# Sample retention in a two-layer decode step: outer products on 128 zero-padded rows, fp32 old-state outputs of four batches side by side

## The chip, the cores and the metric

The kernel runs on one core of a Trainium2 chip. The metric is device time in microseconds (us), the median of several runs of the whole program. TensorE (PE) multiplies, ScalarE (ACT), VectorE (DVE) and GpSimd (POOL) work on elements, SyncE (SP) issues the DMAs.

## The reference, cut to what matters

One step of a hybrid decoder: 512 prompt tokens of one sequence and 8 sample sequences (batches) of 8 tokens each, model width 1024, two layers. Layer 0 mixes tokens by retention with 4 heads, key width 256, value width 512. Both layers then do cross-attention into 256 memory tokens and a gated ConvFFN.

For the 8 sample batches, the chunk is the 8 tokens, and each batch and head has an old state `s` of 256 x 512:

```python
scores = jnp.einsum('bhqd,bhkd->bhqk', qc, kc) * inner
o = jnp.einsum('bhqk,bhkv->bhqv', scores, vc) + jnp.einsum('bhqd,bhdv->bhqv', qc * q_dec, s)
s = s * c_dec + jnp.einsum('bhkd,bhkv->bhdv', kc * k_dec, vc)
```

The output `o` is normalised over its 512 values, multiplied by a gate and projected. The new states go back to memory. So each head reads 8 x 256 x 512 floats (4 MB) of state and writes as many. All results are fp32.

## The kernel before, in words

**Precision.** An fp32 operand is split into a high and a low part in the reduced format F32R (`split`, L190: a cast on ACT, a subtraction on DVE or POOL). A product is three matmuls: high x high, high x low, low x high (`mm3`, L185). Matmuls of plain fp32 operands exist too, in cross-attention's `stacked` (L995) and in the broadcast of the norm's scales.

**Order of the work.** PE runs one main stream of weight tiles (`project`, `run_tasks`): each tile of 512 KB is loaded by SP, cast on ACT, its rest subtracted on DVE, and used by 48 matmuls of 288 columns, shown as `acc<-xhl,wh` and `acc<-xhl,wl`. All else is a side generator that the class `Weave` (L86) puts between steps of the main stream. Weave keeps a planned time `now`: each matmul adds its columns / 2340 us, at least 0.107 (L179), and a side that yields `d` is taken up again when `now` has grown by `d` since it was last resumed; the matmuls of the side itself count as part of that. `join` runs a side to its end at once. PE, ACT, DVE, POOL and SP each take their instructions in the order in which this writes them.

**A head of retention** (`head_tasks`, L750): two weight tiles each for queries and keys, four tiles for values, four for the gate. After the keys `keys_side` (L584) turns them and makes the masked sample scores `As`; after the values `mid_side` (L622) makes the prompt's state, gathers keys and values of the samples with a selection matrix into `kst` and `vst` (L638 to L645) and makes the prompt's score products (`khl` by `qhl`, L653). It starts `b_side` (L660) for the samples. After the gate `out_side` (L710) makes the prompt's outputs. The next head's key evacuation joins both of them (L774) and writes the decayed sample queries to `Z` (L775). For the last head, the output projection joins them (L854).

**`b_side`** takes the 16 half states of a head (8 batches, two key halves of 128) in the order u = 2 b + k2. `load` fetches a half state of 128 x 512 into one of 7 buffers `S`, six ahead. `prep` splits it: cast `Sh` on ACT (L192), rest `Sl` on POOL (L193), two ahead. Per update there are three matmuls: the outer product of 8 tokens' keys and values, which stand on 32 rows of `kst`/`vst` (24 rows carry the three products of the split, row strip 32 g) (L695), and `Z` times `Sh` and times `Sl` into one output `pso` (L697). `Z` has 128 columns per update: 64 of the high part, 64 of the low, all zero but for the batch's own tokens. Then DVE makes the new state in place (L699) and SP stores it (L700); the side yields 1.9. The outputs thus stand on 128 partitions, high and low, are added (L703, L704), normalised on 64 rows and handed to `gate_out` (L569).

PSUM has four one-bank buffers `tp` for all sides in this stage, and two larger ones for the main stream.

Of the kernel before, what the change touches and what calls it, by code (L numbers as in the profile page):

```python
# [135 lines left out]
def body(ctx, tc, a, cdec):  # L136
# [4 lines left out]
    def f(t):  # L141
        return t.bitcast(F32)
# [393 lines left out]
    xs = new(ap1, [128, KT, 128], "xs", F32R)  # L536
    for hl in range(2):
        pool.tensor_copy(xs[:, :, 64 * hl:64 * hl + 64], f(xhl[:, hl, :, 0:NS]))
    Z = new(ap, [128, 2, 1088], "Z", F32R)
    pool.memset(f(Z), 0.0)  # L540
    Zv = Z.rearrange("p k (b s) -> p k b s", s=136)
    AOFF = (0, 512, 896, 1152)
    hd = [dict() for _ in range(H)]
    y3 = {}

    def rope_evac(i, ps, s):
        p = flat(ps)
# [18 lines left out]
        rstd_pow(rs[:rows], mv[:rows, 1:2], 1, rows, ap, 1.0, GN_EPS)  # L566
        return mv, rs

    def gate_out(h, on, rows, c0):  # L569
        ps = tp()  # L570
        sg = hd[h]["sg"]
        for i in range(4):
            transpose(ps[:, rows * i:rows * (i + 1)], on[:rows, 128 * i:128 * i + 128], ident[:rows, :rows])
        y = new(ap, [128, 4, 128], "yt", bufs=2)
        dve.tensor_tensor(out=y[:, :, :rows], in0=ps[:, :4 * rows].rearrange("p (i t) -> p i t", i=4),
                          in1=sg[:, :, c0:c0 + rows], op=ALU.mult)
        if h < 3:
            dma.dma_start(out=y_dram[:, 4 * h:4 * h + 4, c0:c0 + rows], in_=y[:, :, :rows])
        else:
            for i2 in range(2):  # L580
                t = y3[i2]
                split(t[:, 0, :, c0:c0 + rows], t[:, 1, :, c0:c0 + rows], y[:, 2 * i2:2 * i2 + 2, :rows])

    def keys_side(h):  # L584

        s = hd[h]
        r, khl, qhl = s["rk"], s["khl"], s["qhl"]
        yield 4.5
        ks = new(ap, [128, 2, 128], "ks", F32R)
        for hl in range(2):  # L590
            pool.tensor_copy(ks[:, :, 64 * hl:64 * hl + 64], f(khl[:, hl, :, 0:NS]))
        s["kt_s"] = kt_s = new(ap, [NS, 2, 256], "kt_s", F32R)
        ps = tp()
        for k2 in range(2):
            transpose(ps[:NS, 128 * k2:128 * k2 + 128], r[:, k2, 0:NS], ident)
        split(kt_s[:, 0], kt_s[:, 1], ps[:NS, 0:256], scale=tab[:NS, 528 + h:529 + h])
        yield 1.0
        s["kd"] = kd = new(ap1, [128, 2, 4, 256], "kdA", F32R)
        for c2 in range(2):
            ps = tp()  # L600
            for j in range(2):
                c = 2 * c2 + j
                for k2 in range(2):
                    transpose(ps[:, 256 * j + 128 * k2:256 * j + 128 * k2 + 128],
                              r[:, k2, NS + 128 * c:NS + 128 * c + 128], ident)
            for j in range(2):
                c = 2 * c2 + j
                split(kd[:, 0, c], kd[:, 1, c], ps[:, 256 * j:256 * j + 256],
                      scale=tab[:, 512 + 4 * h + c:512 + 4 * h + c + 1])
            yield 1.5  # L610
        ps = tp()
        for k2 in range(2):
            for hl in range(2):
                mm(ps[:, :NS], ks[:, k2], qhl[:, hl, k2, 0:NS], k2 + hl == 0, k2 + hl == 2)
        t1 = new(ap, [NS, NS], "sc1", bufs=2)
        act.copy(t1, ps[64:128, :NS])
        dve.tensor_tensor(out=t1, in0=ps[0:64, :NS], in1=t1, op=ALU.add)
        dve.tensor_tensor(out=t1, in0=t1, in1=tab[:NS, 256 + 64 * h:320 + 64 * h], op=ALU.mult)
        s["As"] = As = new(ap, [NS, 128], "As", F32R)
        split(As[:, 0:64], As[:, 64:128], t1)  # L620

    def mid_side(h):  # L622

# [3 lines left out]
        for k2 in range(2):  # L627
            ps = tp()
            for c in range(4):
                cc = slice(128 * k2, 128 * k2 + 128)  # L630
                mm3(ps, kd[:, 0, c, cc], kd[:, 1, c, cc], vhl[:, 0, c], vhl[:, 1, c], c == 0, c == 3)
                yield 0.0
            sp = new(ap, [128, DV], "S", bufs=7)
            act.copy(sp, ps)
            dma.dma_start(out=a["o_ret_p"][0, 0, h, 128 * k2:128 * k2 + 128], in_=sp)
        s["kst"] = kst = new(ap, [128, 2, 256], "kst", F32R)
        s["vst"] = vst = new(ap, [128, 2, DV], "vst", F32R)
        for w, (src, dst, n) in enumerate(((kt_s, kst, 256), (vs, vst, DV))):  # L638
            for j in range(2):
                ps = tp()  # L640
                rr = slice(32 * j, 32 * j + 32)
                for hl in range(2):
                    mm(ps[:, :n], sel[rr, 2 * w + hl], src[rr, hl], hl == 0, hl == 1)
                act.copy(dst[:, j], ps[:, :n])
            yield 0.5  # L645
        s["bl"] = wv.spawn(b_side(h), 0.5)
        s["A"] = A = new(ap1, [128, 2, 1280], "kdA", F32R)
# [12 lines left out]
    def b_side(h):  # L660

        s = hd[h]
        As, vs, kst, vst = s["As"], s["vs"], s["kst"], s["vst"]
        S, hl_ = {}, {}

        def state(t, u):
            return t[0, u // 2, h, 128 * (u % 2):128 * (u % 2) + 128]

        def load(u):
            if u < 2 * B:  # L670
                S[u] = new(ap, [128, DV], "S", bufs=7)
                dma.dma_start(out=S[u], in_=state(a["state_ret"], u))

        def prep(u):
            if u < 2 * B:
                hl_[u] = [new(ap, [128, DV], t, F32R, bufs=3) for t in ("Sh", "Sl")]
                split(*hl_[u], S[u], lo_pool=True)

        for u in range(7 - 1):
            load(u)  # L680
        yield 3.5
        prep(0)
        yield 1.0
        prep(1)
        pso = tp()
        for hl in range(2):
            mm(pso, As, vs[:, hl], hl == 0, False)
        yield 0.3
        for u in range(2 * B):
            load(u + 7 - 1)  # L690
            prep(u + 2)
            b, k2 = divmod(u, 2)
            g, j = b % 4, b // 4
            psu = tp()
            mm(psu, kst[32 * g:32 * g + 32, j, 128 * k2:128 * k2 + 128], vst[32 * g:32 * g + 32, j], True, True)  # L695
            for i, t in enumerate(hl_.pop(u)):
                mm(pso, Z[:, k2, 128 * b:128 * b + 128], t, False, u == 2 * B - 1 and i == 1)  # L697
            Su = S.pop(u)
            dve.scalar_tensor_tensor(out=Su, in0=Su, scalar=cdec[h], in1=psu, op0=ALU.mult, op1=ALU.add)  # L699
            dma.dma_start(out=state(a["o_ret_s"], u), in_=Su)  # L700
            yield 1.9
        t0 = new(ap, [NS, DV], "At", bufs=2)
        act.copy(t0, pso[64:128])  # L703
        dve.tensor_tensor(out=t0, in0=pso[0:64], in1=t0, op=ALU.add)  # L704
        mv, rs = gn_stats(t0, NS)
        dve.tensor_scalar(out=t0, in0=t0, scalar1=mv[:NS, 0:1], scalar2=rs[:NS], op0=ALU.subtract, op1=ALU.mult)
        yield 5.5
        gate_out(h, t0, NS, 0)

    def out_side(h):  # L710

        s = hd[h]
        A, vhl = s["A"], s["vhl"]
        ons = {}
        for qc in range(5):
            if qc < 4:
                ps = tp()
                for kc in range(qc + 1):
                    o = AOFF[kc] + 128 * (qc - kc)
                    mm3(ps, A[:, 0, o:o + 128], A[:, 1, o:o + 128], vhl[:, 0, kc], vhl[:, 1, kc], kc == 0, kc == qc)  # L720
                mv, rs = gn_stats(ps, 128)
                ons[qc] = on = new(ap, [128, 512], "on", bufs=2)
                nb = new(ap, [128, 1], "gn_nb", bufs=3)
                dve.tensor_scalar(out=nb, in0=mv[:, 0:1], scalar1=rs, scalar2=-1.0, op0=ALU.mult, op1=ALU.mult)
                act.activation(on, ps, AF.Identity, scale=rs, bias=nb)
                yield 6.0
            if qc > 0:
                gate_out(h, ons.pop(qc - 1), 128, NS + 128 * (qc - 1))
                yield 0.5

    def xk0(kt):
# [18 lines left out]
    def head_tasks(h):  # L750
# [16 lines left out]
        def ev_k(i, ps):  # L767
            rope_evac(i, ps, sk_)
            if i == 1:
                s["rk"] = sk_["r"]  # L770
                s["khl"] = khl = new(ap1, [128, 2, 2, NT], "khl", F32R)
                split(khl[:, 0], khl[:, 1], sk_["r"])
                if h > 0:
                    wv.join(hd[h - 1]["bl"], hd[h - 1]["out"])  # L774
                split(Zv[:, :, :, 0:8], Zv[:, :, :, 64:72], s["tq"].rearrange("p k (b t) -> p k b t", t=T))  # L775
                s["keys"] = wv.spawn(keys_side(h))

        tasks = project([(w_in, 256 * h), (w_in, 256 * h + 128)], xk0, ev_q)
# [1 line left out]
        for kp in range(4):  # L780
            def run(wt, kp=kp):
# [29 lines left out]
                t0 = new(ap, [NS, DV], "At", bufs=2)  # L811
                act.copy(t0, pvs[64:128])
                dve.tensor_tensor(out=t0, in0=pvs[0:64], in1=t0, op=ALU.add)
                split(vs[:, 0], vs[:, 1], t0, scale=rtok[:NS, 0:1])
                s["mid"] = wv.spawn(mid_side(h), 1.5)
                if h == 3:
                    s["y2"] = wv.spawn(y2_side())
# [652 lines left out]
```

## Time and profile before

| | us |
|---|---|
| median of three runs | 1966.99 (1962.16 to 1967.77) |
| the profiled execution | 1960.34 |
| its span, first to last instruction | 1958.5 |
| PE busy in the span | 1905.7 |
| DVE, ACT, POOL busy | 1095.6, 757.0, 400.9 |

A row of a timeline gives the start, the time to the end of the last of its instructions, engine, line of the helper that records the instruction (L176 for matmuls, L182 for transposes, L192 and L193 for splits), operation, out<-in by tile names, partitions x columns, and the count. Matmuls overlap, so the cost of one to the stream is read from the distance of starts, not from its duration. A stationary operand is written as rows*columns (32*128: 32 rows, 128 output columns).

### The profile page before, as it was taken

The page shows a single profiled execution, that of the slowest core. Times are in us where ns is not written, and L with a number is a line of the kernel's source. Part 1 is how long each engine was busy: PE and PEld are TensorE (multiplying, and loading weights), DVE is VectorE, ACT ScalarE, POOL GpSimd, SP SyncE. Part 2 cuts the span into 40 slices and gives each one's busy share as a digit, 9 for nine tenths or more (in the row PEclk, how much of TensorE's full clock was granted, in tenths as well). Part 3 has the DMA queues.
Part 4 walks back from the last instruction along what each step waited for, and adds up shares of the span by engine and source line. Part 5 has one row for each costly group of instructions (what it writes and reads, how often), then busy time and mean ns, then how long its engine had stood idle before and what let it go on. Part 6 is the DMA issues. An engine that isn't in the chain of part 4 may idle for free. (4 is left out here: it accounts for less than half of the span.)

```text
span 1958.5 us, 32666 instructions
## 1 busy us (share of the span) xinstructions
PE 1905.7 (97%) x13341; PEld 1772.8 (91%) x13341; DVE 1095.6 (56%) x1651; ACT 757.0 (39%) x1142; POOL 400.9 (20%) x491
## 2 busy tenths in 40 slices
PE   7999999999999999999999999978999999999998
PEld 5888888888899989899999999858888999999998
DVE  4645546354542554576366356696545664564467
ACT  5443342434522434443134234435443432342235
POOL 0123142231400321221011011354212110110010
PEclk9999999999999999999999999989999999999999
DMA  8635363454642464323222222446453332222224
GB/s 276 204 115 187 91 204 109 147 156 145 213 147 87 151 200 147 116 87 86 77 87 83 80 87 70 147 134 203 147 189 101 86 86 77 87 84 79 87 71 138
DMA packets 309293, 247.96 MB, mean 127 GB/s; under 512 B 12248, under 2 KB 268104, under 8 KB 309143
## 3 DMA queue, kind: packets, MB, share of 16 engines
q1 hardware_dynamic: 309143, 245.87, 41.0%
q8 instruction: 105, 1.72, 0.4%
q14 instruction: 45, 0.37, 0.1%
HBM read 208.95 MB, written 36.88 MB: 126 GB/s over the span
## 5 line engine op out<-in xcount | busy, mean ns | idle before, releaser
L176 PE MATMUL acc<-xhl,wh 128*128 128x288 f32 x4608 | 931.7, 297 | 1.5 <-DVE r L552 1.2
L176 PEld LDWEIGHTS acc<-xhl,wh 128*128 128x128 f32 x4608 | 742.3, 188 | 12.8 <-issue 2.7
L176 PE MATMUL acc<-xhl,wl 128*128 128x288 f32 x2304 | 678.4, 295 | 0.0
L192 ACT CAST wh<-wraw 128x1024 fp32r<-128x1024 f32 (+2 forms) x276 | 281.5, 1025 | 573.4 <-PE acc L176 464.4
L176 PEld LDWEIGHTS acc<-xhl,wl 128*128 128x128 f32 x2304 | 433.7, 188 | 0.0
L193 DVE TENSOR_TENSOR wl<-wraw,wh 128x1024 fp32r<-128x1024 f32 (+1 forms) x223 | 271.2, 1220 | 115.4 <-ACT wh L192 111.8
L176 PE MATMUL acc<-yhl,wh 128*128 128x288 f32 (+2 forms) x1408 | 284.0, 297 | 0.1
L176 PEld LDWEIGHTS acc<-yhl,wh 128*128 128x128 f32 x1408 | 225.6, 188 | 0.5 <-ACT yhl L192 0.4
L176 PE MATMUL acc<-yhl,wl 128*128 128x288 f32 (+2 forms) x704 | 206.9, 294 | 0.0
L193 POOL TENSOR_TENSOR wl<-wraw,wh 128x1024 fp32r<-128x1024 f32 (+1 forms) x53 | 129.9, 2454 | 276.1 <-ACT wh L192 269.0
L1182 DVE SCALAR_TENSOR_TENSOR c<-e,cw,c 128x592 f32<-128x592 f32 x176 | 145.9, 831 | 3.9 <-ACT c L1180 0.3
L379 DVE TENSOR_TENSOR x<-x,acc 128x576 f32<-128x576 f32 x64 | 48.2, 753 | 159.4 <-PE acc L176 159.3
L176 PEld LDWEIGHTS acc<-yhl,wl 128*128 128x128 f32 x704 | 132.5, 188 | 0.0
L193 POOL TENSOR_TENSOR Sl<-S,Sh 128x512 fp32r<-128x512 f32 x64 | 82.2, 1287 | 203.4 <-ACT Sh L192 203.0
L176 PE MATMUL acc<-qo,wh 128*128 128x288 f32 x512 | 109.9, 308 | 6.3 <-DVE x L1110 6.1
L1176 POOL COPY cb<-e 128x16 f32<-128x16 f32 x88 | 18.8, 214 | 444.7 <-DVE e L1173 444.7
L176 PE MATMUL acc<-wh,mT 128*128 128x512 f32 x256 | 91.4, 426 | 5.3 <-ACT wh L192 5.3
L176 PEld LDWEIGHTS acc<-qo,wh 128*128 128x128 f32 x512 | 83.0, 193 | 13.1 <-DVE x L1110 7.8
L1173 DVE TENSOR_TENSOR e<-acc,rstd_bc 128x64 f32<-128x64 f32 x88 | 19.5, 222 | 127.2 <-PE acc L176 121.4
L176 PE MATMUL acc<-wh,xhl 128*128 128x512 f32 x256 | 85.5, 400 | 0.0
L1180 ACT ACTIVATE c<-e,cw 128x592 f32<-128x592 f32 x88 | 77.6, 884 | 17.4 <-DVE e L1175 16.3
L699 DVE SCALAR_TENSOR_TENSOR S<-S,tp 128x512 f32<-128x512 f32 x64 | 43.7, 683 | 59.4 <-PE tp L176 41.9
(282 smaller groups left out, 2526.4 us busy)
## 6 DMA issues: line engine op xcount, KB each, us to landing
wraw<-in_w_up SPq DMA_DIRECT2D x88, 512.0 KB, 3.9
wraw<-in_w_ret_in SPq DMA_DIRECT2D x48, 512.0 KB, 4.0
S<-in_state_ret SPq DMA_DIRECT2D x64, 256.0 KB, 3.2
o_ret_s<-S SPq DMA_DIRECT2D x64, 256.0 KB, 3.2
kvr<-in_cache_mem_k SPq DMA_DIRECT2D x64, 256.0 KB, 5.1
kvr<-in_cache_mem_v SPq DMA_DIRECT2D x64, 256.0 KB, 3.4
wraw<-in_w_down SPq DMA_DIRECT2D x32, 512.0 KB, 4.2
wraw<-in_w_down SPq DMA_DIRECT2D x24, 384.0 KB, 3.5
```

The costliest lines, as they stand in the source:

```text
L176: i = nc.tensor.matmul(out, lhsT, rhs, start=start, stop=stop)
L192: act.copy(hi, src)
L193: (pool if lo_pool else dve).tensor_tensor(out=lo, in0=src, in1=f(hi), op=ALU.subtract)
L379: dve.tensor_tensor(out=x[:, i], in0=x[:, i], in1=flat(ps), op=ALU.add)
L699: dve.scalar_tensor_tensor(out=Su, in0=Su, scalar=cdec[h], in1=psu, op0=ALU.mult, op1=ALU.add)
L1173: dve.tensor_tensor(out=ev[:, 0:8, 2:10], in0=ps[:, A0:A0 + NS].rearrange("p (b t) -> p b t", t=T), in1=rstd_bc[:, 0:NS].rearrange("p (b t ...
L1176: pool.tensor_copy(cb[:, 0:16, j].rearrange("p (b t) -> p b t", t=2), ev[:, 0:8, 8:10])
L1180: act.activation(c, e[:, 2:2 + n], AF.Identity, scale=cw[:, 2, j:j + 1], bias=cw[:, 3, j:j + 1])
L1182: dve.scalar_tensor_tensor(out=c, in0=e[:, i:i + n], scalar=cw[:, i, j:j + 1], in1=c, op0=ALU.mult, op1=ALU.add)
```

## The change

In `b_side` the outer product works on all 128 rows: `kst` becomes one persistent buffer for all heads, with a block of 128 rows per batch that holds zeros but for the batch's own 32 rows. Those are filled by four copies of 32 rows where one copy of 128 rows stood. The old states are no longer split. The output of an old state is a matmul in plain fp32 with 32 columns of `Z`, and four batches (j = 0 to 3, in the four column strips, so on PSUM partitions 32 j) follow each other directly; batches 0 to 3 use the first 8 of the 32 rows, batches 4 to 7 the next 8. The states go in the order (half of the batches, key half, batch). `As` is laid out likewise, with zeros, and is one fp32 matmul with `vs32`, the unsplit sample values. The output stands on 128 rows, of which 64 carry tokens; it is normalised by the same function as the prompt's, `normed`, and `gate_out` picks out the rows. Ten state buffers, eight loads ahead; the load of u + 8 stands behind the store of u. The yield falls from 1.9 to 1.7.

```diff
-    Z = new(ap, [128, 2, 1088], "Z", F32R)
-    pool.memset(f(Z), 0.0)
-    Zv = Z.rearrange("p k (b s) -> p k b s", s=136)
+    Z = new(ap, [128, 2, 272], "Z")
+    pool.memset(Z, 0.0)
+    Zv = Z.rearrange("p k (g r) -> p k g r", r=136)[:, :, :, 0:128].rearrange("p k g (j s) -> p k g j s", s=32)[:, :, :, :, 0:T]
+    kst = new(ap, [128, B, 256], "kst", F32R)
+    pool.memset(f(kst), 0.0)
+    As = new(ap, [NS, 128], "As")
+    pool.memset(As, 0.0)
...
+    def normed(o):
+        mv, rs = gn_stats(o, 128)
+        on = new(ap, [128, 512], "on", bufs=2)
+        nb = new(ap, [128, 1], "gn_nb", bufs=3)
+        dve.tensor_scalar(out=nb, in0=mv[:, 0:1], scalar1=rs, scalar2=-1.0, op0=ALU.mult, op1=ALU.mult)
+        act.activation(on, o, AF.Identity, scale=rs, bias=nb)
+        return on
...
-        s["As"] = As = new(ap, [NS, 128], "As", F32R)
-        split(As[:, 0:64], As[:, 64:128], t1)
+        pool.tensor_copy(As.rearrange("p (j s) -> p j s", s=32)[:, :, 0:16].rearrange("p j (g t) -> p g j t", t=T),
+                         t1.rearrange("p (g j t) -> p g j t", g=2, t=T))
...
-                act.copy(dst[:, j], ps[:, :n])
+                if w:
+                    act.copy(vst[:, j], ps[:, :n])
+                    continue
+                for g in range(4):
+                    act.copy(kst[32 * g:32 * g + 32, 4 * j + g], ps[32 * g:32 * g + 32, :n])
...
+        order = [(4 * g + j, k2) for g in range(2) for k2 in range(2) for j in range(4)]
...
-        def prep(u):
-            if u < 2 * B:
-                hl_[u] = [new(ap, [128, DV], t, F32R, bufs=3) for t in ("Sh", "Sl")]
-                split(*hl_[u], S[u], lo_pool=True)
-        for u in range(7 - 1):
+        for u in range(8):
             load(u)
-        yield 3.5
-        prep(0)
-        yield 1.0
-        prep(1)
+        yield 4.5
         pso = tp()
-        for hl in range(2):
-            mm(pso, As, vs[:, hl], hl == 0, False)
+        mm(pso, As, s["vs32"], True, False)
         yield 0.3
         for u in range(2 * B):
-            load(u + 7 - 1)
-            prep(u + 2)
-            b, k2 = divmod(u, 2)
-            g, j = b % 4, b // 4
+            b, k2 = order[u]
+            if u % 4 == 0:
+                for j in range(4):
+                    c = 128 * (b // 4) + 32 * j
+                    mm(pso[32 * j:32 * j + 32], Z[:, k2, c:c + 32], S[u + j], False, u == 2 * B - 4)
             psu = tp()
-            mm(psu, kst[32 * g:32 * g + 32, j, 128 * k2:128 * k2 + 128], vst[32 * g:32 * g + 32, j], True, True)
-            for i, t in enumerate(hl_.pop(u)):
-                mm(pso, Z[:, k2, 128 * b:128 * b + 128], t, False, u == 2 * B - 1 and i == 1)
+            mm(psu, kst[:, b, 128 * k2:128 * k2 + 128], vst[:, b // 4], True, True)
             Su = S.pop(u)
             dve.scalar_tensor_tensor(out=Su, in0=Su, scalar=cdec[h], in1=psu, op0=ALU.mult, op1=ALU.add)
             dma.dma_start(out=state(a["o_ret_s"], u), in_=Su)
-            yield 1.9
-        t0 = new(ap, [NS, DV], "At", bufs=2)
-        act.copy(t0, pso[64:128])
-        dve.tensor_tensor(out=t0, in0=pso[0:64], in1=t0, op=ALU.add)
-        mv, rs = gn_stats(t0, NS)
-        dve.tensor_scalar(out=t0, in0=t0, scalar1=mv[:NS, 0:1], scalar2=rs[:NS], op0=ALU.subtract, op1=ALU.mult)
-        yield 5.5
-        gate_out(h, t0, NS, 0)
+            load(u + 8)
+            yield 1.7
+        on = normed(pso)
+        yield 6.0
+        gate_out(h, on, 0)
...
-                split(Zv[:, :, :, 0:8], Zv[:, :, :, 64:72], s["tq"].rearrange("p k (b t) -> p k b t", t=T))
+                for k2 in range(2):
+                    pool.tensor_copy(Zv[:, k2], s["tq"][:, k2].rearrange("p (g j t) -> p g j t", g=2, t=T))
...
-                split(vs[:, 0], vs[:, 1], t0, scale=rtok[:NS, 0:1])
+                s["vs32"] = vs32 = new(ap, [NS, DV], "vs32")
+                act.activation(vs32, t0, AF.Copy, scale=rtok[:NS, 0:1])
+                split(vs[:, 0], vs[:, 1], vs32)
```

In `gate_out` the four transposes take all 128 rows, and for the sample rows two DVE multiplications (one per group of four batches) pick the token columns out of the transposed tile.

## Rows read from the trace of the kernel before

**Rows 1.** Part 1 and part 2 of the page.

```profile
PE 1905.7 (97%) x13341; PEld 1772.8 (91%) x13341; DVE 1095.6 (56%) x1651; ACT 757.0 (39%) x1142; POOL 400.9 (20%) x491
...
PEclk9999999999999999999999999989999999999999
```

**Rows 2.** Windows of the span: busy us and instructions per engine, PEclk, DMA.

```profile
143.40:184.90 41.50, 41.50 (x230) 33.43 (x229) 18.27 (x31) 17.41 (x27) 19.87 (x18) 1.00 0.65 208
184.90:260.30 75.40, 75.39 (x438) 65.78 (x438) 39.71 (x59) 28.30 (x43) 16.06 (x14) 1.00 0.36 108
```

**Rows 3.** Timeline of PE, 547.9 to 560.2 (start, us, ..., [idle before]).

```profile
557.98 0.53 PE L176 MATMUL acc<-qhl,wh 128*128 128x288 f32 x2 [0.69 <-ACT qhl L192]
...
559.41 0.40 PE L176 MATMUL acc<-qhl,wh 128*128 128x288 f32 x1 [0.90 <-DVE qhl L193]
```

**Rows 4.** Timeline of PE, 145.6 to 147.4.

```profile
145.89 0.29 PE L176 MATMUL acc<-xhl,wl 128*128 128x288 f32 x1
146.11 0.50 PE L176 MATMUL tp<-vst,kst 32*128 32x512 f32 x1
146.54 0.50 PE L176 MATMUL tp<-Sh,Z 128*128 128x512 f32 x1
146.88 0.40 PE L176 MATMUL tp<-Sl,Z 128*128 128x512 f32 x1
147.11 0.42 PE L176 MATMUL acc<-xhl,wh 128*128 128x288 f32 x2
147.38 0.30 PE L176 MATMUL acc<-xhl,wl 128*128 128x288 f32 x1
```

**Rows 5.** Timeline of PE, 478.4 to 485.6.

```profile
478.48 5.65 PE L176 MATMUL tp<-vhl,kdA 128*128 128x512 f32 x24
484.06 0.51 PE L176 MATMUL tp<-kt_s,sel 32*128 32x256 f32 x4
```

**Rows 6.** Timeline of PE in cross-attention, 718.4 to 720.4.

```profile
718.56 0.29 PE L176 MATMUL acc<-xhl,wl 128*128 128x288 f32 x1
718.78 1.07 PE L176 MATMUL tp<-kvr,Z 128*32 128x256 f32 x16
719.78 0.54 PE L176 MATMUL acc<-xhl,wh 128*128 128x288 f32 x2
720.15 0.30 PE L176 MATMUL acc<-xhl,wl 128*128 128x288 f32 x1
```

**Rows 7.** Timeline of PE, 718.70 to 718.83.

```profile
718.78 0.42 PE L176 MATMUL tp<-kvr,Z 128*32 128x256 f32 x4
```

**Rows 8.** Timeline of PE, 493.0 to 494.9.

```profile
493.38 0.73 PE L176 MATMUL tp<-vs,As 64*128 64x512 f32 x2
494.04 0.50 PE L176 MATMUL tp<-vst,kst 32*128 32x512 f32 x1
```

**Rows 9.** Timeline of PE, 653.2 to 654.9.

```profile
653.32 1.52 PE L176 MATMUL tp<-qt,ones 64*128 64x64 f32 x10
654.60 0.51 PE L176 MATMUL acc<-xhl,wh 128*128 128x288 f32 x2
```

**Rows 10.** Groups of PE by line and form, the transposes of the gate.

```profile
L182 PE MATMUL tp<-ident,on 128*128 128x128 f32 x64 | 9.8, 275 | 0.0
...
L182 PE MATMUL tp<-ident,At 64*128 64x64 f32 x16 | 1.8, 234 | 0.0
```

**Rows 11.** Groups by line and form, all engines, 120 to 560.

```profile
L193 POOL TENSOR_TENSOR Sl<-S,Sh 128x512 fp32r<-128x512 f32 x64 | 82.2, 1287 | 203.4 <-ACT Sh L192 203.0
...
L192 ACT CAST Sh<-S 128x512 fp32r<-128x512 f32 x64 | 39.7, 621 | 63.3 <-PE tp L176 43.8 <-POOL Sl L193 15.5 <-DMA S<-in_state_ret 2.0
```

**Rows 12.** Timeline of all engines, 474 to 498.

```profile
484.65 0.66 ACT L644 CAST kst<-tp 128x256 fp32r<-128x256 f32 x2
...
486.15 2.72 PE L176 MATMUL tp<-qhl,khl 128*128 128x512 f32 x12
```

**Rows 13.** Part 6 of the page, DMA issues (count, KB each, us to landing).

```profile
S<-in_state_ret SPq DMA_DIRECT2D x64, 256.0 KB, 3.2
```

More of the change, by code (lines that the diff above doesn't have):

```diff
@@ L567, in gn_stats, with gate_out @@
         return mv, rs
-    def gate_out(h, on, rows, c0):
+    def gate_out(h, on, c0):
         ps = tp()
@@ L572, in gate_out @@
         for i in range(4):
-            transpose(ps[:, rows * i:rows * (i + 1)], on[:rows, 128 * i:128 * i + 128], ident[:rows, :rows])
+            transpose(ps[:, 128 * i:128 * (i + 1)], on[:, 128 * i:128 * i + 128], ident)
         y = new(ap, [128, 4, 128], "yt", bufs=2)
-        dve.tensor_tensor(out=y[:, :, :rows], in0=ps[:, :4 * rows].rearrange("p (i t) -> p i t", i=4),
-                          in1=sg[:, :, c0:c0 + rows], op=ALU.mult)
+        psv = ps.rearrange("p (i t) -> p i t", i=4)
+        n = 128
+        if c0:
+            dve.tensor_tensor(out=y, in0=psv, in1=sg[:, :, c0:c0 + n], op=ALU.mult)
+        else:
+            n = NS
+            for g in range(2):
+                dve.tensor_tensor(out=y[:, :, 32 * g:32 * g + 32].rearrange("p i (j t) -> p i j t", t=T),
+                                  in0=psv.rearrange("p i (j s) -> p i j s", s=32)[:, :, :, 8 * g:8 * g + T],
+                                  in1=sg[:, :, 32 * g:32 * g + 32].rearrange("p i (j t) -> p i j t", t=T), op=ALU.mult)
         if h < 3:
-            dma.dma_start(out=y_dram[:, 4 * h:4 * h + 4, c0:c0 + rows], in_=y[:, :, :rows])
+            dma.dma_start(out=y_dram[:, 4 * h:4 * h + 4, c0:c0 + n], in_=y[:, :, :n])
         else:
@@ L581, in gate_out @@
                 t = y3[i2]
-                split(t[:, 0, :, c0:c0 + rows], t[:, 1, :, c0:c0 + rows], y[:, 2 * i2:2 * i2 + 2, :rows])
+                split(t[:, 0, :, c0:c0 + n], t[:, 1, :, c0:c0 + n], y[:, 2 * i2:2 * i2 + 2, :n])
+    def normed(o):
[5 more added lines that the diff above has]
+        return on
     def keys_side(h):
@@ L632, in mid_side @@
                 yield 0.0
-            sp = new(ap, [128, DV], "S", bufs=7)
+            sp = new(ap, [128, DV], "S", bufs=10)
             act.copy(sp, ps)
             dma.dma_start(out=a["o_ret_p"][0, 0, h, 128 * k2:128 * k2 + 128], in_=sp)
-        s["kst"] = kst = new(ap, [128, 2, 256], "kst", F32R)
         s["vst"] = vst = new(ap, [128, 2, DV], "vst", F32R)
-        for w, (src, dst, n) in enumerate(((kt_s, kst, 256), (vs, vst, DV))):
+        for w, (src, n) in enumerate(((kt_s, 256), (vs, DV))):
             for j in range(2):
@@ L662, in b_side @@
         s = hd[h]
-        As, vs, kst, vst = s["As"], s["vs"], s["kst"], s["vst"]
-        S, hl_ = {}, {}
+        vst = s["vst"]
+        S = {}
+        order = [(4 * g + j, k2) for g in range(2) for k2 in range(2) for j in range(4)]
         def state(t, u):
-            return t[0, u // 2, h, 128 * (u % 2):128 * (u % 2) + 128]
+            b, k2 = order[u]
+            return t[0, b, h, 128 * k2:128 * k2 + 128]
         def load(u):
             if u < 2 * B:
-                S[u] = new(ap, [128, DV], "S", bufs=7)
+                S[u] = new(ap, [128, DV], "S", bufs=10)
                 dma.dma_start(out=S[u], in_=state(a["state_ret"], u))
-        def prep(u):
-            if u < 2 * B:
-                hl_[u] = [new(ap, [128, DV], t, F32R, bufs=3) for t in ("Sh", "Sl")]
-                split(*hl_[u], S[u], lo_pool=True)
-        for u in range(7 - 1):
+        for u in range(8):
             load(u)
-        yield 3.5
-        prep(0)
-        yield 1.0
-        prep(1)
+        yield 4.5
         pso = tp()
-        for hl in range(2):
-            mm(pso, As, vs[:, hl], hl == 0, False)
+        mm(pso, As, s["vs32"], True, False)
         yield 0.3
         for u in range(2 * B):
-            load(u + 7 - 1)
-            prep(u + 2)
-            b, k2 = divmod(u, 2)
-            g, j = b % 4, b // 4
+            b, k2 = order[u]
+            if u % 4 == 0:
+                for j in range(4):
+                    c = 128 * (b // 4) + 32 * j
+                    mm(pso[32 * j:32 * j + 32], Z[:, k2, c:c + 32], S[u + j], False, u == 2 * B - 4)
             psu = tp()
-            mm(psu, kst[32 * g:32 * g + 32, j, 128 * k2:128 * k2 + 128], vst[32 * g:32 * g + 32, j], True, True)
-            for i, t in enumerate(hl_.pop(u)):
-                mm(pso, Z[:, k2, 128 * b:128 * b + 128], t, False, u == 2 * B - 1 and i == 1)
+            mm(psu, kst[:, b, 128 * k2:128 * k2 + 128], vst[:, b // 4], True, True)
             Su = S.pop(u)
@@ L720, in out_side @@
                     mm3(ps, A[:, 0, o:o + 128], A[:, 1, o:o + 128], vhl[:, 0, kc], vhl[:, 1, kc], kc == 0, kc == qc)
[L721 to L725, printed above, removed]
+                ons[qc] = normed(ps)
                 yield 6.0
             if qc > 0:
-                gate_out(h, ons.pop(qc - 1), 128, NS + 128 * (qc - 1))
+                gate_out(h, ons.pop(qc - 1), NS + 128 * (qc - 1))
                 yield 0.5
```

## The prediction, made before the change ran

> **What bounds the kernel now.** I began with the engine totals and the slices of the page: TensorE (PE) is busy 97% of the span and its granted clock stays near full speed, 2.4 GHz, throughout [rows 1]. Busy time of pipelined matmuls overstates, so I then looked at the retention stage by stretches. Head 0's sixteen state updates run from 143.4 to 184.9 us, and in these 41.5 us PE is never idle while ACT and POOL work less than half the time and the DMA engines 0.65 [rows 2]. The same holds until the next head's updates at 260.3. In the whole of retention PE stops only twice for something visible, 0.69 and 0.90 us near 558 us, behind the last head's gated output [rows 3]. So this stage lasts as long as PE's instruction stream. What PE no longer issues is gained in full, unless a supplier becomes late; what ACT and POOL no longer do is worth nothing by itself.
>
> PE's durations overlap, so I price by starts. The plain stream starts a 288-column matmul each 0.13 us (two in the 0.27 us from 147.11 to 147.38) [rows 4].
>
> **Term 1, one state update of before.** Four heads have sixteen updates each, 64 in all, of three matmuls. The last ordinary matmul starts at 145.89; then come the outer product on 32 rows (146.11), the high and the low half of the old state (146.54, 146.88), and the ordinary stream again at 147.11 [rows 4]. From 145.89 to 147.11 is 1.22 us; less the 0.13 us that the ordinary matmul itself takes, 1.09 us. Three full-array matmuls of 512 columns at 0.23 us each (24 of them between 478.48 and 484.06, 5.58/24 [rows 5]) would be 0.70 us, so about 0.4 us of it is change between a 32-row and a 128-row array. 64 x 1.09 = 69.8 us leave.
>
> **Term 2, the outer products of after.** On 128 rows, zeros included, it is the shape of [rows 5]: 0.23 us, no array change. 64 x 0.23 = 14.7 us come.
>
> **Term 3, the old-state outputs.** Four matmuls in plain fp32 with 32 output columns each, 16 such groups. Cross-attention already does this with 256 moving columns: from 718.56 to 720.15 a group of eight goes by (its first start 718.78, next full-array start 719.78) [rows 6]. In 1.59 us lie, besides the group, three ordinary matmuls (one at 718.56, two at 719.78), 0.39 us: the group costs 1.20 us with both array changes. It leaves 16 records, two per matmul, and four of them start within 0.05 us [rows 7], so the four column strips do run side by side. Retention's group has half as many matmuls of twice the columns: the same 1,024 columns per strip and pass pair, again 1.20 us. 16 x 1.20 = 19.2 us come. Bounds: below, the same without its two changes, about 1.0 us (16.0); above, strips that don't overlap at 512 columns, a rival below. I take 1.20, the row with the same form.
>
> By the Trainium skill (FP8 and Floating Point Precision, TensorE Precision Notes), true fp32 makes four passes through the array, against one for the reduced form that the split used. Taken alone, without the overlap of strips, that speaks against the change; the trace shows both the dearer fp32 and an overlap that pays for it, and the rule's own result is the rival named below.
>
> **Term 4, small PE items.** The within-chunk score output was two 64-row matmuls, 493.38 to the next start at 494.04, 0.66 us [rows 8]; it becomes one fp32 matmul of 512 columns. Full-array fp32 shows in the broadcast of the norm's scales: ten records of 2 x 64 and 8 x 128 = 1,152 columns in 1.28 us (653.32 to 654.60) [rows 9], or 1.11 ns per column, so 2 x 512 columns take 1.14 us, and perhaps 0.1 us more of array change since the main stream now comes between: +0.6 us a head, 2.4 us. The sample gate's four transposes grow from 64 to 128 columns: 234 against 275 ns [rows 10], at most 0.2 us a head, and they lose a 64-row array change of about the same size; 0.
>
> **Work off PE.** Gone are 64 casts of 0.62 us on ACT and 64 subtractions of 1.29 us on POOL [rows 11]; they lay beside PE, so nothing is booked. Added per head: six more copies of the keys on ACT, two of which now take 0.66 us together [rows 12], so eight need about 2.6 us; one more scaled copy and one cast of the sample values; POOL's strided copies of the scores and of the queries instead of splits. If these were late, the score products of mid_side behind them would wait for a PSUM buffer: the first needs the one that the first four copies empty. That is some 484.65 + 4 x 0.33 = 486.0 us, and before the first score product started at 486.15 [rows 12], so it fits with little to spare; 0 us, at worst the 2 us by which the copies grow, per head. The one memset becomes three on POOL, at the start of the stage, ahead of the first evacuations and long before kst is read. The final normalisation moves from two PSUM reads to a scale-and-bias on ACT; only the gate waits for it, 6.0 units of work later.
>
> **Loads and order.** Eight states instead of six go ahead, the load of u+8 is issued behind the store of u and needs a buffer whose store is two updates old, so SP has less to stand for. But a group now wants four states at once. Its fourth was requested five updates earlier, over 11 us at the present 2.6 us each (41.5 / 16), and a state lands in 3.2 us [rows 13]: hidden, with DMA at 0.65 [rows 2]. If not, PE waits 16 times for what is missing. The Weave books 1.7 per update instead of 1.9 but less own matmul work, so about ten steps of the main stream fall to four updates instead of eight; the updates spread over a similar time, and the joins with the next head come after it. At the last head the join is just reached when the gate is ready; the two waits of [rows 3] may grow by the 2 to 3 us that a normalisation takes. I book 0.
>
> **Sum.** 69.8 - 14.7 - 19.2 - 2.4 = 33.5 us less. The profiled execution took 1960.34 us (span 1958.5), so 1927 us of its own; the median of the three runs lies 6.6 us higher, 1966.99, from which 33.5 gives **1933 us**, 1.7% less.
>
> **Rivals.**
> - *Given back in waits* (0.15). PE's stream is shorter, but stands at the PSUM buffers of mid_side (4 x 2 us), at the last join (3 us) and at one or two groups' states: 11 to 16 us return, 1944 to 1949. For it: the tight 486.0 against 486.15 and the existing waits of [rows 3]. Against it: not one wait in the updates now, and less work on ACT.
> - *Slower: strips one after another* (0.03). If at 512 columns the four column strips of a group queue for the array, each costs an fp32 matmul of its own, 1.14 us by [rows 9]; a group 4.6 + 0.2 = 4.8 us, 16 of them 76.8. Then 76.8 + 14.7 + 2.4 - 69.8 = +24 us, 1991. It decides for slower where a group passes (69.8 - 14.7 - 2.4) / 16 = 3.3 us. Against it: four starts within 0.05 us [rows 7]. The Trainium skill's four passes at 0.23 us [rows 5] would give 3.7 us, a group of 3.7 + 0.2, and 1977 us; no row here supports it with strips in line.
> - *No change* (0.04). The updates' cost is really set by a supplier, and the stage keeps its pace. That would need PE idle time that the trace hides inside its modelled ends; the evenly spaced starts of 0.13 us [rows 4] speak against it. 1964 to 1967.
>
> **Numbers.** The forecast has 0.78. Its own spread: group at 1.0 instead of 1.2 (-3 us), the small pauses after ACT and POOL let go of shared work (-3 us), runs 6 us apart; from 1924 to 1940. Reaching to most of the give-back cases makes 1924 to 1947; left out are the slower case and no change. A measurement of this kernel tells 0.3%, about 6 us, from no change. Faster: 0.78 + 0.15; same 0.04; slower 0.03.
>
> **What would show it.** Right: the outer products are 128-row matmuls 0.23 us apart from the next start; the 16 groups leave 128 records, eight each, of some 1.0 us from first start to the next full-array start; casts and subtractions of states gone; a head's period, now 116.9 us (143.4 to 260.3 [rows 2]), about 8 us shorter, and the rest of the span unchanged. Wrong: starts of a group 1 us apart (strips in line), idle PE in front of a group behind a state's load, in front of the score products behind key copies, or a gap near the last join of more than 3 us.

## The result, and the profile after

The changed kernel takes 1938.41 us, the median of four runs (1936.67 to 1941.59); the kernel before took 1967.38 beside it. The ratio is 0.986, interval [0.9843, 0.9876]: 29.0 us less. Run again later beside fresh runs of before, it took 1940.48 against 1964.92, 0.9871 [0.9853, 0.9889]: 24.4 us less. Forecast were 33.5 us less and 1933.

The profiled execution took 1938.62 us. Part 1 and the clock line of part 2 of its page, which answer to [rows 1]:

```profile
PE 1879.1 (97%) x13341; PEld 1756.7 (91%) x13341; DVE 1082.4 (56%) x1643; ACT 729.3 (38%) x1098; POOL 324.9 (17%) x441
...
PEclk9999999999999999999999999989999999999999
```

PE loses 26.6 us of busy time with the same 13341 records (32-column fp32 matmuls leave two each, which happens to make up for those removed). ACT and POOL lose 27.7 and 76.0, which is no gain by itself.

Next, the updates of head 0 on PE, 143.9 to 147.0 us, the stretch that answers to [rows 4]:

```profile
144.24 0.29 PE L176 MATMUL acc<-xhl,wl 128*128 128x288 f32 x1
144.47 1.07 PE L176 MATMUL tp<-S,Z 128*32 128x512 f32 x8
145.46 0.50 PE L176 MATMUL tp<-vst,kst 128*128 128x512 f32 x1
145.81 0.43 PE L176 MATMUL acc<-xhl,wh 128*128 128x288 f32 x2
...
146.46 0.30 PE L176 MATMUL acc<-xhl,wl 128*128 128x288 f32 x1
146.60 0.39 PE L176 MATMUL tp<-vst,kst 128*128 128x512 f32 x1
146.83 0.42 PE L176 MATMUL acc<-xhl,wh 128*128 128x288 f32 x2
```

Read it by starts, as before. From 144.24 to 145.81 are 1.57 us. Less the ordinary matmul at 144.24 (0.13) and the first outer product (0.24), the group of four strips costs **1.20 us**, the value taken from cross-attention in [rows 6]. A lone outer product goes by from 146.60 to 146.83: **0.23 us**, the value of [rows 5].

The same engine where the old-state output is opened, before the first update of head 0, answering to [rows 8]:

```profile
142.21 0.29 PE L176 MATMUL acc<-xhl,wl 128*128 128x288 f32 x1
142.43 1.12 PE L176 MATMUL tp<-vs,As 64*128 64x512 f32 x2
143.49 0.40 PE L176 MATMUL acc<-xhl,wh 128*128 128x288 f32 x1
```

From 142.43 to 143.49 is 1.06 us, with 0.09 us of entry ahead of it (142.43 - 142.21 - 0.13); [rows 8] had 0.66. Term 4 (+0.6 a head) was right too, within 0.2. The same score output starts at 142.79 in the trace of before:

```profile
142.79 0.73 PE L176 MATMUL tp<-vs,As 64*128 64x512 f32 x2
```

A head as a whole, from one head's first sample score to the next one's. First after, then before (start:end and length, then busy us and instructions of PE, PEld, DVE, ACT and POOL, granted clock, DMA share, GB/s):

```profile
142.40:252.20 109.80, 108.52 (x668) 93.48 (x667) 55.30 (x87) 38.30 (x58) 17.56 (x20) 1.00 0.49 153
```

```profile
142.80:259.70 116.90, 116.89 (x668) 99.23 (x667) 57.98 (x90) 45.70 (x70) 35.94 (x32) 1.00 0.46 143
```

A period falls by 7.1 us, where "about 8" was forecast. The difference stands in the PE column: before, PE had 0.01 us of idle time, now 1.28. PE's waits in the whole of retention, 100 to 560 us (waiting operation, what it waited for, us in total, times, longest):

```profile
PE tp L182 <- ACT on L606: 4.2, 4, 1.3
PE acc L176 <- ACT qhl L192: 2.5, 1, 2.5
```

Together 6.6 us, where before had 1.6 [rows 3]. They are the transposes of the sample gate, once per head, and the last join.

**Where the time went.** The matmul that stalls at the last join starts at 557.98 in before [rows 3] and at 530.12 after: 27.9 us earlier. The first score output already starts 0.36 us earlier (142.43 against 142.79), and what lies ahead of it is no part of the change, so 27.5 us lie between the two. By then after has waited 6.63 us (three times 1.28, 0.34 and 2.45) and before 0.69. PE's stream itself thus became 27.5 + 6.63 - 0.69 = **33.4 us shorter**; the sum said 33.5. All that is missing was given back.

The gate first. DVE in head 0, 185 to 194 us (in square brackets the engine's idle time before the row and what ended it):

```profile
185.67 0.67 DVE L571 BATCH_NORM_STATS2 gn_st<-tp 128x6 f32<-128x512 f32 x1
...
186.31 0.75 DVE L562 TENSOR_TENSOR rt<-acc,cs 128x576 f32<-128x576 f32 x1
...
188.66 1.43 DVE L778 TENSOR_TENSOR tq<-r,tab 128x64 f32<-128x64 f32 x1 [0.73 <-POOL r L564]
190.01 1.21 DVE L193 TENSOR_TENSOR wl<-wraw,wh 128x1024 fp32r<-128x1024 f32 x1
...
191.32 0.17 DVE L572 BATCH_NORM_AGGREGATE gn_mv<-gn_st 128x2 f32<-128x6 f32 x1
...
192.19 1.35 DVE L193 TENSOR_TENSOR qhl<-r,qhl 128x1152 fp32r<-128x1152 f32 x1
193.46 0.21 DVE L605 TENSOR_SCALAR gn_nb<-gn_mv,gn_rs 128x1 f32<-128x1 f32 x1
```

The statistics of the sample output are taken at 185.67, but their aggregate stands at 191.32. Between them, in the order in which DVE took its instructions, lie the rotation of the next head's queries, the decayed sample queries, and the low part of a weight tile. The bias `gn_nb` stands behind one more subtraction of 1.35 us. In the kernel's text `normed` has statistics, aggregate, `rp_v` and `gn_nb` directly one behind the other. So the engines do not simply take their instructions in the order of the text, as the section on the kernel before has it; what sets the order on DVE no run here shows. Only behind `gn_nb` can ACT write `on`, and PE arrives 1.28 us too early:

```profile
194.61 0.66 PE L182 MATMUL tp<-ident,on 128*128 128x128 f32 x4 [1.28 <-ACT on L606]
```

The last join comes second. PE, 526.2 to 534.5 us, answering to [rows 3]:

```profile
526.22 0.66 PE L182 MATMUL tp<-ident,on 128*128 128x128 f32 x4 [0.34 <-ACT on L606]
...
530.12 0.86 PE L176 MATMUL acc<-qhl,wh 128*128 128x288 f32 x3 [2.45 <-ACT qhl L192]
530.81 0.40 PE L176 MATMUL acc<-qhl,wl 128*128 128x288 f32 x1
531.01 0.68 PE L176 MATMUL acc<-qhl,wh 128*128 128x288 f32 x2
531.49 0.44 PE L176 MATMUL acc<-qhl,wl 128*128 128x288 f32 x1
...
534.33 0.30 PE L176 MATMUL acc<-khl,wl 128*128 128x288 f32 x1
```

The two waits of before, 0.69 and 0.90, became 0.34 and 2.45. From 531.01 to 531.49 two matmuls take 0.48 us, 0.24 each instead of 0.13: PE's clock has fallen to half. The window over that stretch shows it (columns as above; 0.50 is the granted clock, that is 1.2 GHz):

```profile
531.00:533.00 2.00, 2.00 (x10) 2.00 (x10) 0.00 (x0) 0.00 (x0) 0.00 (x0) 0.50 0.00 0
```

Before, the clock stayed at 1.00 behind its shorter waits. The account up to 534.33: 33.4 gained, 3.84 given back at three gates, 1.2 more at the join (0.34 + 2.45 - 0.69 - 0.90), and what is left, 1.4, to the half clock. The same matmul starts at 561.64 before, so from the first score output to it **the stage** takes 418.9 us before (561.64 - 142.79) and 391.9 after (534.33 - 142.43): **27.0 us** remain. These two matmuls stand at the same places of the stream in every kernel below, with 1,734 `acc` matmuls between them, and "the stage" is the time between their starts.

The profiled pair differs by only 21.7 us, while the medians differ by 24.4 and 29.0. Most of what the pair lacks lies in a later stage that the change does not touch, the pooling stage. First the stretch of after, then the same 381 PE records of before:

```profile
1228.00:1326.20 98.20, 81.49 (x381) 68.55 (x380) 87.12 (x108) 45.42 (x82) 52.56 (x30) 0.87 0.51 165
```

```profile
1254.90:1348.40 93.50, 76.43 (x381) 62.82 (x380) 86.76 (x109) 45.16 (x83) 52.78 (x30) 0.93 0.51 161
```

Here PE works with gaps, its granted clock changes between the two levels, and the same work took 98.2 us at 0.87 and 93.5 at 0.93. Single executions of before lay between 1959.07 and 1971.80. What one execution pair says of 5 us is therefore no evidence; the retention stage, at clock 1.00, can be compared row by row.

### The profile page after: what moved, and what is told of

Its sections match the earlier page's. It is cut to its first block, busy times and chain, and to the rows that moved or that the text cites. A ratio compares the mean times of both kernels' runs of the same rounds, so it can differ in the third digit from the quotient of the medians.

```text
span 1936.8 us, 32464 instructions
## 1 busy us (share of the span) xinstructions
PE 1879.1 (97%) x13341; PEld 1756.7 (91%) x13341; DVE 1082.4 (56%) x1643; ACT 729.3 (38%) x1098; POOL 324.9 (17%) x441
## 5 line engine op out<-in xcount | busy, mean ns | idle before, releaser
L176 PE MATMUL acc<-qo,wl 128*128 128x288 f32 x256 | 75.5, 298 | 0.0
```

The lines of the kernel that those rows point to most:

```text
L176: i = nc.tensor.matmul(out, lhsT, rhs, start=start, stop=stop)
```

## The experiments

Theory: the stream of PE sets the stage; padding saves array changes, strips side by side pay for plain fp32, and work taken off ACT and POOL is worth nothing. Rival: a good part comes from the shorter supply of the updates. The first four kernels ran beside one set of runs of before (median 1964.71, 18 runs), the other four beside another (1964.92, 9 runs). The changed kernel stands at 1938.41 us for the first set, though it ran beside other runs of before (1967.38), and at 1940.48 for the second, beside which it ran. The stage is free of that: it takes 391.9 us in the first trace of the changed kernel and 391.2 in the second.

### The outer product on 32 rows again

```diff
-            mm(psu, kst[:, b, 128 * k2:128 * k2 + 128], vst[:, b // 4], True, True)
+            g = 32 * (b % 4)
+            mm(psu, kst[g:g + 32, b // 4, 128 * k2:128 * k2 + 128], vst[g:g + 32, b // 4], True, True)
```

`kst` is filled by one copy of 128 rows as in before.

> The changed kernel with the outer products back on 32 rows (keys gathered into the old small buffer by one copy each); the fp32 strips stay. Theory (the gain is what TensorE no longer issues, priced by starts): in the trace of before, a lone 32-row matmul costs 0.10 us of entry, 0.43 us to the next start and 0.11 us more at the first full-array matmul behind it, 0.64 us against 0.24 us on 128 rows; 64 x 0.40 = 25 us come back, about 1963 us. So the padding would be most of the whole gain. Rival (the gain comes from the unsplit states, that is from fewer matmuls and from the casts and subtractions that ACT and POOL lose): little comes back, 1940 to 1948 us.

Measured: 1958.88 us, 0.9975 [0.9956, 0.9995], so 20.5 us more than the changed kernel. PE around one update of head 0:

```profile
150.65 0.29 PE L176 MATMUL acc<-xhl,wl 128*128 128x288 f32 x1
150.88 0.50 PE L176 MATMUL tp<-vst,kst 32*128 32x512 f32 x1
151.31 0.53 PE L176 MATMUL acc<-xhl,wh 128*128 128x288 f32 x2
151.68 0.30 PE L176 MATMUL acc<-xhl,wl 128*128 128x288 f32 x1
```

From 150.65 to 151.31, less 0.13, is 0.53 us, and the two matmuls after it take 0.37 instead of 0.26: 0.64 us, against 0.23 with zeros. But sixteen of the 64 outer products stand directly behind a group of strips and share its way back to the full array; there a group and its product take 1.65 us instead of 1.57 and the two matmuls behind them 0.37 instead of 0.26, some 0.2 us more. 48 x 0.41 + 16 x 0.2 = 22.9 us, a little above what was measured: 20.5 us by the medians, 20.6 by the stage (412.5 us). Padding is worth that much in this order.

### The padding alone, on the kernel before

```diff
+    kst = new(ap, [128, B, 256], "kst", F32R)
+    pool.memset(f(kst), 0.0)
...
-            mm(psu, kst[32 * g:32 * g + 32, j, 128 * k2:128 * k2 + 128], vst[32 * g:32 * g + 32, j], True, True)
+            mm(psu, kst[:, b, 128 * k2:128 * k2 + 128], vst[:, j], True, True)
```

To make room, `S` has 6 buffers, `Sh` and `Sl` 2, and splitting runs one update ahead instead of two.

> The kernel before with nothing but the outer products on 128 zero-padded rows; states are still split, three full-array matmuls per update. To fit the memory it has six state buffers instead of seven and splits one update ahead instead of two. Theory: three matmuls of 0.23 us in place of 1.09 us, 64 x 0.39 = 25 us less, about 1942 us, and no wait at the sample gate of three heads, since the normalisation stays as before. Rival (the unsplit states carry the gain): 1958 to 1967 us.

Measured: 1951.77 us, 0.994 [0.9922, 0.9959], 13 us less than before. The stream does what the theory says. PE in one update:

```profile
151.24 0.29 PE L176 MATMUL acc<-xhl,wl 128*128 128x288 f32 x1
151.37 0.39 PE L176 MATMUL tp<-vst,kst 128*128 128x512 f32 x1
151.60 0.40 PE L176 MATMUL tp<-Sh,Z 128*128 128x512 f32 x1
151.84 0.39 PE L176 MATMUL tp<-Sl,Z 128*128 128x512 f32 x1
152.07 0.43 PE L176 MATMUL acc<-xhl,wh 128*128 128x288 f32 x2
```

Three matmuls 0.23 apart, no pause before or after: 0.70 us instead of 1.09 [rows 4], which over 64 updates is 25 us. The stage takes 405.3 us, 13.5 less than before, so some 11 us of the 25 are missing. The states are split later here, and the largest group of PE's waits from 100 to 560 us is for that (columns as above):

```profile
PE tp L176 <- POOL Sl L193: 2.6, 5, 0.8
```

All waits of PE there add up to 6.9 us (before 1.6), and such a wait can cost more than its length: the update at 172.68 takes 2.35 us instead of 0.70 with 1.12 us of idle time in its rows. How the rest of the 11 us divides was not worked out. The arithmetic of the padding is confirmed; the time that it would give with splitting two ahead was not measured. Here the split states' supply does decide, which the change has no need of.

### The gate three units later

```diff
-        yield 6.0
+        yield 9.0 if h < 3 else 6.0
```

> The changed kernel with the sample gate of the first three heads 9.0 instead of 6.0 planned units behind the normalisation. Theory: the waits of 1.28 us in front of the four sample transposes of heads 0 to 2 are the sample normalisation's chain on DVE, queued behind the next head's evacuations; with more time before the gate they go, 3 x 1.28 = 3.8 us, about 1934.5 us, and the trace shows none of them. Rival (they only move, to the prompt's transposes or to the join with the next head): 1937 to 1940 us.

Measured: 1935.74 us, 0.9861 [0.9842, 0.988], 2.7 us less than the changed kernel by the medians of the two sets. All of PE's waits in retention that are left:

```profile
PE acc L176 <- ACT qhl L192: 2.5, 1, 2.5
PE acc L176 <- DVE r L563: 0.5, 1, 0.5
```

The wait for `on` is gone with nothing else changed; DVE takes the chain in the same interleaved order as in the changed kernel, so the gate stood too close behind a chain that had become longer. The 2.7 us are less than two executions can differ by; the stage is the firmer reading: 387.6 us against 391.9 and 391.2, so 3.6 to 4.3 us less, where 3.8 was forecast.

### The casts kept, first try

```diff
+        def prep(u):
+            if u < 2 * B:
+                hl = [new(ap, [128, DV], t, F32R) for t in ("Sh", "Sl")]
+                split(*hl, S[u], lo_pool=True)
```

> The changed kernel, but ACT still casts each half state and POOL still subtracts, into buffers that nothing reads. Theory (what ACT and POOL no longer do is worth nothing, since their work lay beside TensorE's): 1938 to 1941 us, the most by a longer wait at the sample gate, whose normalisation uses POOL too. Rival (the relief of ACT, POOL and the memory ports they share with DVE is part of the gain): 1945 us or more, with longer casts and subtractions of the weights and new idle time of TensorE.

Measured: 1969.28 us, 1.003 [1.001, 1.005]: 31 us *more* than the changed kernel. By its numbers the theory fell. The trace says what else had been put in. ACT, 150 to 160 us:

```profile
150.00 0.62 ACT L192 CAST Sh<-S 128x512 fp32r<-128x512 f32 x1 [1.39 <-POOL Sl L193]
...
158.59 1.04 ACT L192 CAST wh<-wraw 128x1024 fp32r<-128x1024 f32 x1
```

With one buffer each, a cast must wait until POOL has subtracted the one before it; ACT stands 1.4 us at every cast, and the cast of the main stream's weights stands in line behind. PE then waits 7.5 us for `wh` and 8.7 us for a state's update, and the granted clock, 1.00 over head 0 of the changed kernel, is 0.97 there (columns as above):

```profile
142.40:260.00 117.60, 109.69 (x647) 94.08 (x647) 54.20 (x86) 45.20 (x70) 34.74 (x33) 0.97 0.44 135
```

The stage takes 423.6 us, 31.7 more than the changed kernel's. This kernel measured a chain of its own, so the question was put again.

### The changed kernel again

> The changed kernel itself once more, on the chip of the next three, as their measure. Both theories: 1938 us, 1.4% below the kernel before.

Measured: 1940.48 us, 0.9871 [0.9853, 0.9889]. The same two places wait, 3.8 us in all for `on` and 2.5 us for `qhl`. The stage takes 391.2 us.

### The casts kept, without a chain

```diff
+                act.copy(Sh, S[u])
+                pool.tensor_tensor(out=Sl, in0=S[u], in1=S[u], op=ALU.subtract)
```

> The changed kernel with one cast on ACT and one subtraction on POOL per half state again, now without a chain between them: POOL subtracts the state from itself, both write one scratch buffer each that nothing reads. In the run with casts kept, each cast had to wait for the subtraction before it, and the casts of the weights stood behind that. Theory (only this chain cost the 30 us; work beside TensorE's is free): within 4 us of the changed kernel, no idle TensorE in front of weights. Rival (the work itself on ACT, POOL and their shared ports costs): 10 us or more above the changed kernel, with TensorE idle in front of weights' casts.

Measured: 1937.33 us, 0.9865 [0.9845, 0.9885], the same as the changed kernel. The groups by line and form show that the work was there, nearly as long as in [rows 11]:

```profile
L709 POOL TENSOR_TENSOR Sl<-S 128x512 fp32r<-128x512 f32 x64 | 72.7, 1136 | 161.0 <-DMA S<-in_state_ret 159.1
...
L708 ACT CAST Sh<-S 128x512 fp32r<-128x512 f32 x64 | 39.6, 619 | 39.8 <-DMA S<-in_state_ret 38.6
```

The profiled execution was the slowest of the five (1945.46 us), but its stage takes 391.3 us, against 391.2 in the changed kernel beside it. So 112 us of work beside PE cost nothing as long as nobody on PE's path stands behind a wait of it, and the cost of shared ports that the rival names does not show. It is not the casts that made the first try slow but what they waited for. The theory stands.

### The strips apart

```diff
-            if u % 4 == 0:
-                for j in range(4):
-                    c = 128 * (b // 4) + 32 * j
-                    mm(pso[32 * j:32 * j + 32], Z[:, k2, c:c + 32], S[u + j], False, u == 2 * B - 4)
+            j = u % 4
+            c = 128 * (b // 4) + 32 * j
+            mm(pso[32 * j:32 * j + 32], Z[:, k2, c:c + 32], S[u], False, u >= 2 * B - 4)
```

> The changed kernel with each old-state output issued at its own update, so that no two column strips follow each other; the same 64 fp32 matmuls. Theory (four strips in a row run side by side): each now costs a group's whole price of 1.2 us, 64 x 1.2 - 16 x 1.2 = +58 us, about 1996 us, so that unsplit fp32 alone would lose against the split. Rival (the gain of fp32 outputs does not hang on the overlap of strips): 1938 to 1950 us.

Measured: 1989.94 us, 1.0121 [1.0103, 1.014], slower than before and 49.5 us over the changed kernel. PE around one update:

```profile
150.34 0.29 PE L176 MATMUL acc<-xhl,wl 128*128 128x288 f32 x1
150.56 1.04 PE L176 MATMUL tp<-S,Z 128*32 128x512 f32 x2
151.54 0.50 PE L176 MATMUL tp<-vst,kst 128*128 128x512 f32 x1
151.88 0.43 PE L176 MATMUL acc<-xhl,wh 128*128 128x288 f32 x2
```

One strip takes from 150.34 to 151.88, less 0.13 and 0.24: 1.17 us, as much as four together (1.20). 48 more of them are 56 us. Of the changed kernel's waits those for `on`, 3.8 us, are absent here. The one at the last join is there, only later, because the stage is longer:

```profile
581.30 1.06 PE L176 MATMUL acc<-qhl,wh 128*128 128x288 f32 x3 [2.39 <-ACT qhl L192]
```

56 - 3.8 = 52 us, and the stage takes 443.0 us, 51.7 more than in the changed kernel beside it. The medians, at 49.5, include the later stages. Plain fp32 with 32 columns is the dearer form, and only the company of three others makes it the cheaper one.

### Both waits taken out

```diff
-        yield 6.0
+        yield 9.0 if h < 3 else 6.0
...
                 ons[qc] = normed(ps)
-                yield 6.0
+                yield 6.0 if h < 3 else 5.0
```

The second edit, in `out_side`, lets the steps of the last head's prompt output come earlier.

> The changed kernel with the sample gates of heads 0 to 2 at 9.0 instead of 6.0 units, and the last head's prompt outputs paced 5.0 instead of 6.0, so that the last join finds them finished. Theory: gone are 3 x 1.28 us of waits at the gates, 2.45 + 0.34 us at the last join, and the 1.6 us that the half clock behind that wait costs: 8 us less than the changed kernel, about 1930 us, granted clock 1.00 behind the join. Rival (the waits move: the last head's transposes come too early for their normalisation): 1935 to 1938 us.

Measured: 1932.99 us, 0.983 [0.9812, 0.9849], 7.5 us less than the changed kernel beside it, and faster than both kernels. PE's waits in retention, and the window behind the last join:

```profile
PE acc L176 <- DVE r L563: 0.4, 1, 0.4
PE tp L176 <- DVE S L719: 0.2, 1, 0.2
```

```profile
526.00:560.00 34.00, 34.00 (x257) 33.97 (x256) 12.63 (x14) 8.62 (x10) 0.00 (x0) 1.00 0.26 82
```

With no wait ahead of it the clock stays at 1.00, which ties the half clock to the wait. Now the gain is 31.9 us by the medians. The stage takes 383.9 us, 35.0 less than before: the 33.4 us of the shorter stream, and the 1.6 us that before itself waited.

## Why the prediction was right, and where it was not

- **The bound** was read rightly: PE's stream sets the stage. The strongest evidence is the kernel that keeps 112 us of casts and runs no slower. The earlier loads and the shorter yield can have no part in the gain by way of waits, since PE had 0.01 us of idle time in a whole head of before.
- **Terms 1 to 4** held: 0.23 us for an outer product and 1.20 us for a group stand in the trace as forecast, the score output within 0.2 us, and the stream became 33.4 us shorter instead of 33.5. As the terms hold one by one, the near equality of the sums is not luck. The 0.4 us of array change in term 1 was shown by the padding alone (1.09 to 0.70) and by going back to 32 rows (0.23 to 0.64).
- **Loads and key copies** at nothing: right. PE never waited for a state or for a score product's PSUM buffer, though states landed in 3.8 us instead of 3.2.
- **The step that failed** is the zero for the normalisation, "only the gate waits for it, 6.0 units of work later". I counted the units and not the instructions that DVE takes within them. In before the same normalisation followed the first part of the next head's rotation without anything of it between, and lasted 5.2 us, from a copy at 186.5 to its end on DVE at 191.72, 2.3 us ahead of the transposes at 194.02. Now the links of a chain over DVE, POOL, DVE and ACT are spread through that rotation and its subtractions. The chain lasts 8.9 us, from the statistics at 185.67 to the end of `on` at 194.56, and 1.28 us a head come back, three times. The experiment with the gate three units later removed them.
- **The last join** was booked at 0, with the words that its waits "may grow by the 2 to 3 us". They grew by 1.2 us, and the half clock behind the longer one, which the prediction did not have, cost about 1.4 more.
- **The rival of the waits** was half right. It named the join, and its size (11 to 16 us) was twice what came, 6.5; but of its three places two, the PSUM buffers and the states, showed nothing, and the gate was not among them. The forecast's own case remains the better description, with 6.5 us too much gain by the stage (33.5 against 27.0) and 4.5 and 9.1 by the two pairs of medians. Its range, 1924 to 1947, was wide enough to hold most of this rival too, and so did not decide between them; the rows did.
- **The slower rival**, strips one after another, was ruled out by the one group's 1.20 us, and the strips apart show what a strip costs by itself: 1.17 us with its array changes, 0.98 from its start to the next (150.56 to 151.54). Four in line would by that, as an estimate, have cost 3.9 to 4.7 us a group; the point of decision was 3.3. The Trainium skill (TensorE: Matmul & The Clock Gate, Part 3, the table of measured speedups) gives 2.38 times for three column strips of 512 columns. Four strips here gave 4 x 1.17 / 1.20 = 3.9 times; array changes are in both of these, which flatters the ratio.
- On the outer products, the Trainium skill (TensorEngine Tiling (Array Packing), When to Use Tiling) names a contraction of 32 rows as a case for fourfold row tiling. The runs show the other side: a single such product between full-array matmuls took 0.64 us and 0.23 with 96 rows of zeros. In this order nothing else ran beside it; what four such products issued together would take, no run tried.

## What to carry to other kernels

On an engine that never idles, price an edit by the distances of starts, and count the change of array form on either side of a lone small matmul: zeros can be cheaper than a small tile, and small tiles pay when several go together. Then, before booking a moved chain at nothing, ask what each engine takes between its links, and read that order from a trace rather than from the kernel's text; a delay in planned units says nothing of that. Work beside the bound was free here as long as nothing on PE's path stood behind its waits: the casts cost 0 or 31 us depending on whether they had to wait for the subtractions.

## What the runs showed that I had not expected

- A wait of 2.45 us of PE was followed by some 3 us at a granted clock of 0.50, so that a wait cost more than its length; 0.69, 0.90 and 1.28 us were followed by 1.00.
- DVE did not take the instructions of one normalisation in a row, as the kernel's text has them: the aggregate started 5.65 us after the statistics, with other work between.
- In the pooling stage, where PE works with gaps, the granted clock of the same work was 0.87 in one execution and 0.93 in another, and its time 98.2 and 93.5 us.
- A column strip of 32 alone took as long as four side by side, 1.17 and 1.20 us.
